# A decoder layer's MLP written as one row of 128 steps with every engine in a written order, operands loaded one by one, scaling and rectifier in one operation, and a fourth weight buffer in the output projection

## The chip, the core and the metric

The kernel runs on one core of a Trainium2 chip. The metric is device time in microseconds from launch to end, the median of several runs; lower is better. The core has a matrix engine (PE, TensorE), a vector engine (DVE, VectorE), an activation engine (ACT, ScalarE), a general engine (POOL, GpSimd) and a queue engine (SP) that here issues most transfers. Each takes its own instructions strictly in order; they wait for one another through semaphores. TensorE reads operands from on-chip memory and adds up in eight banks of PSUM; a bank must be emptied by another engine before a new sum starts in it.

## The reference

One layer of a hybrid decoder on 1024 positions of width 1024. Three branches (a matrix memory, differential attention, attention into 256 memory rows) make `merged`; the change lies behind them:

```python
x = x + merged @ w_out[l]
h2 = rms_norm(x, norm_mlp_g[l])
x = x + jnp.square(jax.nn.relu(h2 @ w_up[l])) @ w_down[l]
```

`w_up` is 1024 x 4096, `w_down` 4096 x 1024, everything float32.

## The kernel before, in words

Products are taken in a split float format: each float32 operand is kept as a high part (rounded by a cast on ACT) and a low part (the rest, a subtraction on DVE), and a product is three matmuls, high x high, high x low, low x high (`mm3`). A split of a tile is thus one ACT instruction and one DVE instruction behind it.

**Output projection** (end of `tail`'s first half, line 1410 on). Four groups of two output blocks; each group has two weight tiles of 128 x 1024 (`load_w`, line 142), cast and split into the pool `wp2`. Each of its four results is scaled and added to x (line 1416), stored to `x1d`, squared into `ssq` for the norm, and stored as `h` to `h2d`.

**The MLP** computes both matrix products by a scheme with seven products for a 2 x 2 block product in place of eight (`PROD`, line 1176). A *step* takes one weight block (2 x 2 blocks of 128 x 128) and one operand (2 x 2 blocks of 128 x 512): POOL makes four sums of weight blocks (`wino_s`), ACT and DVE split the seven weight forms (`wsp`), and TensorE runs 7 x 3 = 21 matmuls of 512 columns into seven banks. The operand's seven forms are four sums (`wino_t`, three on DVE and one on POOL) and three plain blocks, also split. Seven banks of eight are in use in a pass, and the next pass starts with the eighth (`bank`): from its second product on it needs the banks of the pass before, in their order.

The up-projection (`wino`) has 16 units of four steps; unit 0 is cut in two so that the MLP may start before the last operands exist. At the end of a unit the seven sums are combined into four results (`combine`: one ACT copy and seven DVE additions that read the banks); `use_up` scales each by the row norm (`tensor_mul`, line 1457), applies the rectifier (ACT, line 1458) and the square (ACT, line 1459), and stores the three plain blocks and, a step later, the four sums to `r_d`. The row norm itself is made inside the first steps by small matmuls (`rstd`; its copy `st`, line 1473, empties a bank that the next pass needs).

The down-projection (`down`) has four output groups and 16 passes of four steps, pass p for group p mod 4 with operands p to p+3; operands 16 to 18 are 0 to 2 loaded again, 19 loads in all. An operand is one to three tiles of 1024 to 2048 columns, each split by one ACT and one DVE instruction (`xsplit`). At the end of a pass the seven banks are added into seven accumulators (lines 1617 to 1619, 1637), and after a group's last pass seven more additions close the result, which is stored to `out`.

**What sets the order.** Matmuls of the MLP keep the written order (`self.pinned`). Everything else of the MLP (ACT, DVE, POOL, SP) was put in order by a planner at build time from its own estimates and the written order as priority. Weights have four raw buffers and four split buffers in the up-projection, three and three in the down-projection. The tiles of the down-projection take the memory of the up-projection's tiles as these come free, and those of the up-projection take that of the output projection's.

## Time and profile before

| what | value |
|---|---|
| median of 3 runs | 2248.64 us (2246.41 to 2258.45) |
| profiled execution: its own time | 2249.61 us |
| its span, first to last instruction | 2247.8 us |
| TensorE busy | 2182.6 us, 97% |
| DVE, ACT, POOL busy | 1398.3, 1019.8, 540.4 us |
| MLP on TensorE | from 1595.5 to 2243.8 us |
| mean granted clock of TensorE | 0.993 |

All numbers are from one profiled execution. In lists of instructions the columns are start, length, engine, source line, operation, tile written and tiles read, shape, count; in brackets the idle time of the engine just before and what ended it. In groups by line they are busy time and mean length (ns) of one, then idle time before them and what ended it. Tiles are named by the program: `p` the seven banks, `wo` split weights, `wraw` raw weights, `xo` and `xd` split operands of the up- and the down-projection, `xr` an operand as loaded, `xts` its sums, `acc` accumulators, `w` and `raw` the weights of the other projections. The lines of the helpers (91 matmul, 104, 105 and 115, 116 the split) stand for many places, so tiles are the better guide.

### The profile page before, as it was taken

How to read it: one execution, taken by the hardware profiler on the slowest of the kernel's cores; microseconds unless marked ns; L12 is line 12 of the kernel's file. 1: busy time of each engine (PE TensorE's matmuls, PEld its weight loads, DVE VectorE, ACT ScalarE, POOL GpSimd, SP SyncE). 2: the span in 40 equal slices, each digit the busy share in tenths (PEclk: the TensorE clock that was granted, in tenths of full speed). 3: DMA queues.
4: the chain of work that ended last, by engine and by line, in shares of the span. 5: the costliest groups of instructions: out<-in, count | busy, mean ns of one | idle time of the engine just before them, and what ended most of it. 6: DMA issues, size and time to landing. Idle time of an engine off the chain costs nothing.

```text
span 2247.8 us, 30530 instructions
## 1 busy us (share of the span) xinstructions
PE 2182.6 (97%) x11222; PEld 1877.5 (84%) x11222; DVE 1398.3 (62%) x2627; ACT 1019.8 (45%) x1994; POOL 540.4 (24%) x696
## 2 busy tenths in 40 slices
PE   7999899999999999999999999999899999899999
PEld 5778788988899999999888888887788888688777
DVE  6645366655138888888752232544588777865688
ACT  6533355444236666666542120323445444543232
POOL 2100000000011111111100002202666665665553
PEclk9999999999999999999999999999999999999999
DMA  6013122111311111110133443436445444844434
GB/s 246 20 71 113 44 87 78 54 60 52 119 55 34 34 31 38 38 36 29 61 128 135 134 148 117 141 103 206 153 143 186 151 155 162 296 163 147 154 118 169
DMA packets 113781, 247.89 MB, mean 110 GB/s; under 512 B 11066, under 2 KB 19551, under 8 KB 111583
## 3 DMA queue, kind: packets, MB, share of 16 engines
q1 hardware_dynamic: 111326, 233.36, 31.5%
q10 hardware_dynamic: 2304, 12.58, 1.4%
q8 instruction: 88, 1.44, 0.3%
q14 instruction: 63, 0.51, 0.1%
HBM read 178.76 MB, written 67.14 MB: 109 GB/s over the span
## 4 chain that ended last, share of the span: by engine, by line
PE 68%; DVE 14%; DMA 8%; ACT 5%; issue 2%; POOL 2%; SPq 0%; DVEq 0%; ACTq 0%; POOLq 0%
PE mm L91 40%; PE p L91 18%; PE sc L91 4%; PE tp L94 2%; PE po L91 2%; DVE sc L67 1%; DMA wraw<-in_wdown 1%; ACT dpe L67 1%; DVE wo L105 1%; DVE dpe L67 1%; PE pr L94 1%; DVE draw L67 1%; DVE dst L67 1%; DMA xr<-h_d 1%; DVE w L116 1%
## 5 line engine op out<-in xcount | busy, mean ns | idle before, releaser
L91 PE MATMUL mm<-hT,w 128*128 128x512 f32 x1920 | 466.4, 397 | 0.5 <-ACT gt L488 0.5
L91 PE MATMUL mm<-w,hT 128*128 128x384 f32 (+3 forms) x2496 | 459.3, 330 | 1.9 <-ACT w L115 1.6
L91 PEld LDWEIGHTS mm<-hT,w 128*128 128x128 f32 x1920 | 356.1, 189 | 76.0 <-ACT gt L488 1.7
L91 PEld LDWEIGHTS mm<-w,hT 128*128 128x128 f32 x2496 | 389.6, 189 | 12.1 <-ACT w L115 2.3
L91 PE MATMUL p<-xd,wo 128*128 128x512 f32 x1344 | 313.3, 394 | 16.5 <-DVE acc L1619 9.4
L91 PEld LDWEIGHTS p<-xd,wo 128*128 128x128 f32 x1344 | 253.5, 190 | 76.2 <-DVE acc L1619 12.8
L91 PE MATMUL p<-xo,wo 128*128 128x512 f32 x1344 | 309.5, 392 | 6.2 <-DVE st L1473 4.2
L91 PEld LDWEIGHTS p<-xo,wo 128*128 128x128 f32 x1344 | 253.2, 189 | 61.2 <-ACT pt L1286 4.6
L91 PE MATMUL mm<-kt,w 128*128 128x512 f32 x1152 | 261.8, 389 | 0.5 <-DVE w L116 0.5
L91 PEld LDWEIGHTS mm<-kt,w 128*128 128x128 f32 x1152 | 216.1, 188 | 46.1 <-DVE w L116 1.0
L104 ACT CAST wo<-wraw 128x896 fp32r<-128x896 f32 x122 | 114.9, 942 | 190.3 <-PE p L91 126.8
L105 DVE TENSOR_TENSOR wo<-wraw,wo 128x896 fp32r<-128x896 f32 x122 | 146.2, 1212 | 49.9 <-ACT wo L104 49.8
L1200 POOL TENSOR_TENSOR wraw<-wraw 128x128 f32<-128x128 f32 x128 | 99.0, 773 | 212.3 <-DMA wraw<-in_wdown 132.2
L115 ACT CAST w<-raw 128x256 fp32r<-128x256 f32 (+2 forms) x144 | 86.4, 619 | 140.1 <-PE mm L91 103.7
L67 ACT ACTIVATE dpe<-sc,dst,drr 128x256 f32<-128x256 f32 (+7 forms) x128 | 106.7, 833 | 62.2 <-DVE dst L67 51.6
L116 DVE TENSOR_TENSOR w<-raw,w 128x256 fp32r<-128x256 f32 (+2 forms) x144 | 100.5, 718 | 52.3 <-ACT w L115 52.3
L105 DVE TENSOR_TENSOR xd<-xd 128x1536 fp32r<-128x1536 f32 (+2 forms) x36 | 69.0, 1922 | 70.5 <-ACT xd L104 70.5
L67 DVE CUSTOM_DVE_ANT_0 sc<-sc,tmask 128x256 f32<-128x256 f32 (+7 forms) x128 | 97.0, 758 | 3.6 <-PE sc L91 2.4
L139 POOL TENSOR_SCALAR hss<-hss 128x4 f32<-128x4 f32 x8 | 3.3, 415 | 398.5 <-ACT mscr L767 398.5
L1201 POOL TENSOR_TENSOR wraw<-wraw 128x128 f32<-128x128 f32 x128 | 96.9, 757 | 0.0
L1202 POOL TENSOR_TENSOR wraw<-wraw 128x128 f32<-128x128 f32 x128 | 94.2, 736 | 0.0
L104 ACT CAST xd<-xd 128x1536 fp32r<-128x1536 f32 (+2 forms) x36 | 54.9, 1528 | 73.0 <-DMA xd<-r_d 73.0
(324 smaller groups left out, 3161.1 us busy)
## 6 DMA issues: line engine op xcount, KB each, us to landing
wraw<-in_wup SPq DMA_DIRECT2D x64, 256.0 KB, 3.2
r_d<-xts SPq DMA_DIRECT2D x16, 1024.0 KB, 4.3
wraw<-in_wdown SPq DMA_DIRECT2D x64, 256.0 KB, 3.1
xd<-r_d SPq DMA_DIRECT2D x19, 768.0 KB, 7.6
xd<-r_d SPq DMA_DIRECT2D x14, 1024.0 KB, 6.3
raw<-in_wgate SPq DMA_DIRECT2D x48, 256.0 KB, 3.0
gates<-gt SPq DMA_DIRECT2D x48, 256.0 KB, 2.1
raw<-in_wd SPq DMA_DIRECT2D x32, 384.0 KB, 3.1
```

Source lines behind the costliest of these rows:

```text
L67: return self.tc.keep_in_program_order(f(*a, **k))
L91: self.pin(self.nc.tensor.matmul(out, l, r, start=start, stop=stop))
L94: self.pin(self.nc.tensor.transpose(out, x, self.ident))
L104: self.A.copy(hi, src)
L105: low = lambda: self.V.tensor_sub(lo, src, f32(hi))
L115: nc.scalar.copy(hi, src)
L116: nc.vector.tensor_sub(lo, src, f32(hi))
L139: g.tensor_scalar(r, ss, 1.0 / width, EPS, op0=ALU.mult, op1=ALU.add)
L1200: G.tensor_add(r[:, 4], r[:, 0], r[:, 3])
L1201: G.tensor_sub(r[:, 5], r[:, 4], r[:, 1])
L1202: G.tensor_sub(r[:, 6], r[:, 1], r[:, 0])
```

## The change

- **One row of steps.** `wino`, `down` and their helpers go; one function `mlp` runs the 64 steps of the up-projection and the 64 of the down-projection in one loop with the same banks. All pools are opened at its start, with three split buffers and four raw buffers for weights, and the down-projection's tiles take over pools of the up-projection's by name.
- **Written order.** DVE, ACT, POOL and SP are wrapped in `InOrder` (line 57), which fixes the written order of what they do in the MLP. In step n the order is: the split of weight n+2, the load of raw block n+5, the sums of raw block n+4, then (inside a pass) the work listed for n and closing additions, or (at its end) the emptying of the banks, the work listed for n, closing additions. The first splits and operands 0 to 2 (`un`) are left to the planner.
- **Operands of the down-projection.** Passes get unequal lengths (`PASSES`): 19 passes of one to four steps, so that a new operand is first used every four steps or so and each of the 16 is loaded once. An operand is split in four pieces of two products (the last of one), four to two steps before its use; the load waits for the last use of the operand in its place, or, for the first five, stands at steps 44 and 60 to 63 (`nup` is 64).
- **Closing additions** (`fold`): two per step, 3 to 8 per step at the end.
- **Scaling with rectifier**: one `scalar_tensor_tensor` (maximum with 0, times the norm) for `tensor_mul` and the activation `Relu`. Unit 15's operand sums go to POOL wholly.
- **Output projection**: `wp2` has four buffers (three before), as a ring of named pools, as has `rp2`.
- A constant tile shrinks from 48 to 40 columns.

The core of the diff, new code first:

```diff
+    PASSES = (
+        (0, (0, 1)), (1, (0, 1)), (2, (0, 1, 2)), (3, (0, 1, 2, 3)),
+        (0, (2, 3, 4)), (1, (2, 3, 4, 5)), (2, (3, 4, 5, 6)), (3, (4, 5, 6, 7)),
+        (0, (5, 6, 7, 8)), (1, (6, 7, 8, 9)), (2, (7, 8, 9, 10)), (3, (8, 9, 10, 11)),
+        (0, (9, 10, 11, 12)), (1, (10, 11, 12, 13)), (2, (11, 12, 13, 14)),
+        (0, (13, 14, 15)), (1, (14, 15)), (2, (15,)), (3, (12, 13, 14, 15)),
+    )
...
+        V0, S0, A0, G0 = nc.vector, nc.sync, nc.scalar, nc.gpsimd
+        V, S, A, G = (InOrder(tc, e) for e in (V0, S0, A0, G0))
...
+        wrp, wop = Ring([wr0, wr1, wr2, wr3]), Ring([wop1, wop2, wop3])
...
+        def down_load(q):
...
+            for p_, tag, i, n in pools:
+                t = p_.tile([P, n, 2, 512], F32R, tag=tag, name=self.name("xd"))
+                for c0 in range(0, n, 4):
+                    c1 = min(c0 + 4, n)
+                    S.dma_start(f32(t[:, c0:c1, 1]), self.rd[q, :, i + c0 : i + c1])
+                parts[q] += [t[:, c0 : min(c0 + 2, n)] for c0 in range(0, n, 2)]
...
+        def down_split(q):
+            t = parts[q].pop(0)
+            split(t[:, :, 0], t[:, :, 1], f32(t[:, :, 1]))
...
+        at(nup - 20, lambda: down_load(0))
+        for i in (15, 15, 14, 11, 10):
+            at(nup - i, lambda: down_split(0))
+        for q in range(1, 16):
+            at(nup - 5 + q if q < 5 else n0[q - 4][-1], lambda q=q: down_load(q))
+            for i in (3, 2, 2, 2) if q == 1 else (4, 3, 2, 2):
+                at(n0[q][0] - i, lambda q=q: down_split(q))
+        for g, i in ((0, -8), (1, 1), (2, 4), (3, 8)):
+            at(nup + i, lambda g=g: acc_tiles(g))
...
+        def squares(u, cs):
+            b = hid[u] = xrp.tile([P, 4, 512], F32, tag="xr", name=self.name("rq"))
+            for i in (1, 3, 2, 0):
+                hf = i % 2
+                V.scalar_tensor_tensor(
+                    out=cs[i], in0=cs[i], scalar=0.0, in1=rb[:, hf * 512 : (hf + 1) * 512], op0=ALU.max, op1=ALU.mult
+                )
+                A.activation(b[:, i], cs[i], AF.Square)
+            A.dma_start(self.rd[u, :, 0:3], b[:, 1:4])
...
+        def fold(n):
+            if n >= nup + 57:
+                k = n - nup - 54 + (n >= nup + 60) - (n == nup + 58)
+            else:
+                k = 2
+            for _ in range(min(k, len(ends))):
+                f, x, y = ends.pop(0)
+                V.tensor_add(x, x, y)
+                if f:
+                    S.dma_start(f, x)
...
+                for i in range(len(run)):
+                    m = n - len(run) + 1 + i
+                    wsp()
+                    raw()
+                    wsum(m + 4)
+                if run[-1] != kps[-1]:
                     for f in todo.pop(n, []):
-                        next(f)
...
+                        f()
+                    if n > nup:
+                        fold(n)
...
+                    h = combine(ps, True)
+                    cs = next(h)
+                    next(h)
+                    k = 1 if r in (1, 3) or u == 15 else 0
+                    if k:
+                        at(n + 1, lambda u=u, cs=cs: squares(u, cs))
+                    else:
+                        squares(u, cs)
+                    at(n + 1 + k, lambda u=u: sums_up(u, G if u == 15 else V))
+                    at(n + 2 + k, lambda u=u: store(u))
...
+                if seen[g] == 1:
+                    V.tensor_sub(a3, a3, a5)
+                for j in range(7):
+                    if seen[g] == 1 and j in (0, 2, 3):
+                        A.copy(A_[j], ps[j])
+                    else:
+                        add(A_[j], A_[j], ps[j])
+            for f in todo.pop(n, []):
+                f()
+            fold(n)
...
-                    self.rp = E(name="rp2", bufs=2)
-                    self.wp = E(name="wp2", bufs=3)
+                    self.rp = Ring([E(name=f"rp2{i}", bufs=1) for i in range(2)])
+                    self.wp = Ring([E(name=f"wp2{i}", bufs=1) for i in range(4)])
...
-                        self.V.tensor_mul(cs[i], cs[i], rb[:, hf * 512 : (hf + 1) * 512])
-                        self.A.activation(cs[i], cs[i], AF.Relu)
-                        self.A.activation(b[:, i], cs[i], AF.Square)
...
-            passes = [(p % 4, tuple(range(p, 4 + p))) for p in range(16)]
...
+            self.mlp(one, gl, sp, rb, ssq, lambda *x, **k: c9.enter_context(tc.tile_pool(*x, **k)))
```

515 lines of the change are left out of this document (212 added, 303 removed).

## The prediction

> **What bounds the kernel now.** I read first the window table over the stages from the output projection to the end (columns: length, busy time and instruction count of each engine, granted clock, DMA share, GB/s), then what TensorE waited for, and last the order of time around each gap.
>
> ```profile
> 1520.00:1600.00 80.00, 75.44 (x331) 61.63 (x330) 35.90 (x35) 31.16 (x41) 25.84 (x20) 1.00 0.61 202
> 1600.00:1700.00 100.00, 93.84 (x415) 76.14 (x414) 84.65 (x100) 51.02 (x72) 72.37 (x88) 0.97 0.42 146
> 1700.00:1900.00 200.00, 200.00 (x884) 165.62 (x883) 160.86 (x195) 94.00 (x139) 124.55 (x179) 1.00 0.44 152
> 1900.00:1960.00 60.00, 52.07 (x212) 40.42 (x211) 47.76 (x44) 33.47 (x36) 28.88 (x33) 0.94 0.87 311
> 1960.00:2060.00 100.00, 100.00 (x442) 82.81 (x442) 62.86 (x61) 40.33 (x41) 62.98 (x85) 1.00 0.47 158
> 2060.00:2180.00 120.00, 114.11 (x497) 92.32 (x497) 81.43 (x88) 40.83 (x37) 63.90 (x92) 1.00 0.42 145
> 2180.00:2248.00 68.00, 61.07 (x260) 49.29 (x258) 56.75 (x70) 17.69 (x16) 26.72 (x43) 0.97 0.44 151
> ...
> 1872.20 0.58 ACT L1254 COPY u<-p 128x512 f32<-128x512 f32 x1
> 1891.24 0.57 ACT L1254 COPY u<-p 128x512 f32<-128x512 f32 x1
> ...
> L91 PE MATMUL px<-dg,ones 128*128 128x128 f32 x16 | 2.1, 274 | 0.0
> L91 PE MATMUL px<-ones,ssq 128*128 128x1 f32 x16 | 1.9, 246 | 0.0
> ...
> PE mm L91 <- DVE w L116: 4.6, 2, 3.0
> PE p L91 <- DVE acc L1619: 9.4, 8, 1.8
> ```
>
> TensorE bounds the kernel, so the change is worth the TensorE time now lost and no more. The two copies of one unit and the next lie 19.04 us apart; a unit is 4 steps of 21 matmuls, so a step takes 4.76 us and a matmul 0.2267 us. Unit for unit the second half of the up-projection and the window 1960 to 2060 run at that pace (442 matmuls per 100 us): nothing can be gained there. Against 442 per 100 us the other windows are short by: 1600 to 1700, 442 - (415 - 32 small ones) = 59 matmuls, 13.4 us, less 4.0 us that the small ones take, 9.4 us; 1900 to 1960 (full 266), 54, 12.2 us; 2060 to 2180 (531), 34, 7.7 us; 2180 to TensorE's end at 2243.8 (283), 23, 5.2 us. With the 4.6 us that the output projection waits for its weights this is 39.1 us, the most that can come back.
>
> **The change, part by part.** The sum is made against the profiled execution: 2249.6 us around a span of 2247.8; the median of the runs shown, 2248.6, is 1.0 lower.
>
> *Fourth out-projection buffer.* With three, the second weight tile of a group can be cast only when the tile three before is released, near the end of the group ahead, and then it stands behind an operand's long split:
>
> ```profile
> 1548.61 2.28 DVE L116 TENSOR_TENSOR xo<-xts,xo 128x2048 fp32r<-128x2048 f32 x1
> 1550.42 1.03 ACT L115 CAST w<-raw 128x1024 fp32r<-128x1024 f32 x1
> 1553.15 0.72 PE L91 MATMUL mm<-mh,w 128*128 128x512 f32 x2 [3.00 <-DVE w L116]
> ```
>
> With four the tile can be cast half a group, over 10 us, earlier, and both waits go: 4.6 us to 0 (bounds 0 and 4.6 left, should the planner still set the cast late). What hangs on the end of this stage, the last stores of h and the loads of the operands, moves with it.
>
> *Start, steps 0 to 5.* The bank that step 2 wants is held by the copy `st`, which stood behind the low parts of two weights, and those behind POOL's sums:
>
> ```profile
> 1609.94 1.09 DVE L105 TENSOR_TENSOR wo<-wraw,wo 128x896 fp32r<-128x896 f32 x1 [1.31 <-ACT wo L104]
> 1610.95 0.16 DVE L1473 COPY st<-px 128x8 f32<-128x8 f32 x1
> 1611.25 4.18 PE L91 MATMUL p<-xo,wo 128*128 128x512 f32 x9 [4.17 <-DVE st L1473]
> 1614.38 13.74 PE L91 MATMUL p<-xo,wo 128*128 128x512 f32 x56
> ```
>
> Nine matmuls took 3.1 us after that wait, 1.1 more than their 2.0. In the written order `st` follows only weight 2, whose raw buffer is now free early. The next wait is then the seven copies that empty the first pass: they stand behind the cast of weight 3 on ScalarE, which waits for a raw block whose buffer frees with the output projection. By the rows below, 3.1 us to land, 3.1 of sums, after POOL's last sums of squares, 0.9 and 0.6 for cast and copy make 8 to 12.5 us from the stage's end; it is wanted at 12. Of the 9.4 us in this window about 6 is the start (4.2 wait, 1.1 clock, rest small); I leave 1.5 (bounds 0.5 and 6). The remaining 3.4 us is VectorE's backlog over steps 5 to 19. Its work there is the same but for what is below; over steps 5 to 14 I count 10 low parts at 1.2, 21 combine and 7 part additions at 0.7, 12 scalings and 9 operand sums at 0.8, 48 us in 47.6. A pass end lets it run some 4 us behind, so I leave 2 (bounds 0 and 5).
>
> *Scaling with rectifier.* One scalar_tensor_tensor for a tensor_mul (its own form on two SBUF operands isn't in this trace; on a PSUM operand, below, it takes as long as an addition), and 64 activations of 632 ns, 40 us, leave ScalarE. They were off TensorE's path, hidden under the 200.00 us busy of 200: 0 (bounds -3 and 3: up to 0.2 us on 13 units). What it moves is the cast of the next weight, behind the last square: 0.6 us sooner.
>
> ```profile
> L105 DVE TENSOR_TENSOR wo<-wraw,wo 128x896 fp32r<-128x896 f32 x122 | 146.2, 1212 | 49.9 <-ACT wo L104 49.8
> L104 ACT CAST wo<-wraw 128x896 fp32r<-128x896 f32 x122 | 114.9, 942 | 190.3 <-PE p L91 126.8 <-POOL wraw L1203 45.8 <-POOL wraw L1200 3.8
> L1200 POOL TENSOR_TENSOR wraw<-wraw 128x128 f32<-128x128 f32 x124 | 96.1, 775 | 186.9 <-DMA wraw<-in_wdown 132.2 <-DMA wraw<-in_wup 46.3 <-DVE wo L105 3.2
> L1457 DVE TENSOR_TENSOR c<-c,rb 128x512 f32<-128x512 f32 x30 | 24.9, 829 | 0.5 <-ACT rb L1484 0.5
> L1458 ACT ACTIVATE c<-c 128x512 f32<-128x512 f32 x30 | 19.0, 632 | 61.8 <-DVE c L1457 61.8
> L1183 POOL TENSOR_TENSOR xts<-rq 128x512 f32<-128x512 f32 x16 | 28.1, 1755 | 49.6 <-ACT rq L1459 47.6 <-DMA r_d<-xts 2.0
> L105 DVE TENSOR_TENSOR xd<-xd 128x1024 fp32r<-128x1024 f32 x8 | 11.0, 1382 | 6.6 <-ACT xd L104 6.6
> L104 ACT CAST xd<-xd 128x1024 fp32r<-128x1024 f32 x8 | 8.4, 1049 | 10.1 <-DMA xd<-r_d 10.1
> L1642 DVE TENSOR_TENSOR acc<-acc,acc 128x512 f32<-128x512 f32 x3 | 2.0, 678 | 0.0
> xd<-r_d SPq DMA_DIRECT2D x19, 768.0 KB, 7.6
> wraw<-in_wdown SPq DMA_DIRECT2D x64, 256.0 KB, 3.1
> 2060.64 4.26 DVE L1619 TENSOR_TENSOR acc<-acc,p 128x512 f32<-128x512 f32 x7
> 1598.93 0.69 DVE L1416 SCALAR_TENSOR_TENSOR gl<-mm,gl 128x512 f32<-128x512 f32 x1 [4.05 <-DMA gl<-in_xT]
> ```
>
> *Seam.* Before, four operands (7.3 MB) with their splits come at once while the last unit is combined, at 311 GB/s and 12.2 us lost. Now operand 0 is loaded 20 steps and split 10 to 15 steps ahead, 1 to 4 are loaded over steps 60 to 63 and split in pieces of two products. DMA: steps 61 to 66 want 12.8 MB in 28.6 us; at 311 GB/s they take 41 us, so weights trail by up to 12 us. A raw block is issued three steps, 14.3 us, before its cast and needs 3 us on POOL, so ScalarE is held some 2 to 3 us at a cast, while TensorE's need comes two steps, 9.5 us, later: hidden. Not hidden is the first pass end after two steps. From step 63's start: low part and combine on VectorE to 7.4, three pieces of operand 1 to 10.7, low part 66 to 11.8, four scalings of unit 15 to 14.8. Its last square ends at 15.4, the cast of weight 67 at 16.4, and only then come the copies that empty pass 0: the first at 17.0, where step 66 wants the bank at 15.0 (2.1 late with its signal). The first addition (after low part and the subtraction) ends at 19.1, another 1.3 late: 3.4 us. In this trace such waits drop the clock in three places of four: the windows with 4.2, 1.9 + 1.8 and 2.1 us of waits show 0.97, 0.94 and 0.97 granted, while the 3.0 us wait of the output projection shows 1.00. In the second place 52 matmuls took 14.6 us for 11.8, and I add 2.0: 5.4 us in place of 12.2 (bounds 2 and 10). Unit 15's sums moved to POOL (4 at 1.755, 7 us, behind sums 69) delay weights 70 to 72 by that much and not past their need.
>
> ```profile
> 1919.42 1.20 PE L91 MATMUL p<-xd,wo 128*128 128x512 f32 x3 [1.92 <-DVE c L1258]
> 1922.43 14.59 PE L91 MATMUL p<-xd,wo 128*128 128x512 f32 x52 [1.81 <-DVE u L1260]
> 2185.17 27.06 PE L91 MATMUL p<-xd,wo 128*128 128x512 f32 x111 [2.09 <-DVE acc L1637]
> ```
>
> [...]
>
> *Middle of the down-projection.* Before, splits of 1536 and 2048 columns stand ahead of the additions that empty the banks (the eight waits for L1619). Now 16 operands are loaded instead of 19, four steps apart, and the emptying follows its step's low part directly. For four steps VectorE has 4 x 1.2 + 3 x 1.3 + 0.7 + 7 x 0.61 = 13.7 us of 19.0. Three more passes (19 for 16) are 21 more additions, 13 us, inside that slack. SP waits for TensorE's last use before each operand load, with the next raw block behind it: 7.6 + 3.1 us to landing and 3 on POOL is 13.7, before its cast at 14.3. I leave 1 of 7.7 (bounds 0 and 5).
>
> *End.* Three groups finish in steps 120, 122 and 123, with 21 additions and 18 of the 21 closing ones (0.68 each) ahead of the low part of weight 127:
>
> ```profile
> 2235.04 8.72 PE L91 MATMUL p<-xd,wo 128*128 128x512 f32 x37 [0.60 <-DVE wo L105]
> ```
>
> From step 122's start: cast and low part 124 to 2.2, seven additions to 6.5, three closing ones to 8.5, low part 125 to 9.6, seven to 13.9, five to 17.3, low part 126 to 18.4, seven to 23.2, low part 127 to 24.3. Steps 126 and 127 run as one, so TensorE wants it at 19.0 + 1.1 = 20.1: 4.2 us late by means, 2.8 at the shortest durations. I take 3.5 and 1.0 for the clock: 4.5 of 5.2 stays (bounds 1 and 8). The close after TensorE's end is unchanged.
>
> Sum left: 0 + 1.5 + 2 + 0 + 5.4 + 1 + 4.5 = 14.4; 39.1 - 14.4 = 24.7; 2249.6 - 24.7 = 2224.9, by the median 2224.
>
> **Rivals.** *Pass ends give it back:* 18 pass ends each wait like the eight before (9.4 / 8 = 1.2 us), 21.6 us where I have 6.4: 2239. For it: engines in a fixed order can't step round a late cast; against it: the 5 us a period of slack. *Slower:* in the up-projection the cast of a unit's fourth weight now always stands behind the four squares, and has three buffers instead of four. From the start of a unit's last step the chain is 12.2 us (low part, 7 combine steps, 4 scalings, square, cast, low part), need at 14.3, slack 2.1. If POOL's sums hold VectorE's two-operand work back more than the 829 ns row shows, each us over the slack costs 1 us on 13 units; from 2 us over, 26 us, it eats the gain, and at 3 over it gives 2224 + 39 = 2263. Against it: the unbroken 200 us, with the same VectorE work. *No loss left:* VectorE runs ahead everywhere but at the seam, 4 us left: 2249 - 35 = 2214, at best 2210. *The buffer and the start do nothing:* 4.6 + 4.5 more, 2233, inside my own range.
>
> **How the numbers follow.** Own case (2216 to 2234) 0.61, nothing left (below 2216) 0.13, pass ends (2234 to 2248) 0.19, slower 0.07. A change under 0.5%, 11 us, can't be told here. Faster than that is below 2237.4: 0.61 + 0.13 and a third of the pass ends, 0.80; same 0.13; slower 0.07. All low ends together leave 0.5 us (2210), all high ones 37 (2247), which doesn't happen at once; range 2210 to 2243.
>
> **What would show it.** No wait of `mm` for `w`; the copy `st` within 2 us of its small matmuls; the up-projection at 19.04 us a unit; the largest remaining wait of TensorE at step 66, behind the squares, and the next at the last weight's low part; no wait over 1 us between. Wrong, if a wait recurs once a unit, if the operands' DMA holds TensorE itself, or if the stalls at the pass ends add up to more than 10 us.

## The result

The changed kernel takes 2230.4 us (median of four, 2225.6 to 2233.3) where the kernel before takes 2249.6 (median of the four beside it): a ratio of 0.9911, 95% interval 0.9884 to 0.9938. The forecast was 2224 us with a range of 2210 to 2243. So the sign and the range held, and the gain is 19 us where 25 were forecast.

The profiled execution of the changed kernel happens to be its fastest, 2225.6 us around a span of 2223.7. That it meets the forecast to 2 us is luck. The first matmul of the output projection comes 5.9 us sooner in it than before (1497.3 for 1503.2), and over the eleven profiles with the same code ahead of it that moment lies anywhere from 1497.3 to 1504.5. The change reaches this earlier code at one point: `wp2` also holds the weights of the three branch projections ahead. With three buffers TensorE waits for these 0.5 us in before, 0.9 in e9 and 1.4 in e1 (both runs below); with four it doesn't wait. The rest of the 5.9 us is spread. So I compare lengths of stages, which don't carry that shift: the output projection, from its first matmul to the first one of the MLP; *up*, from there to the copy `u` of the last hidden unit in step 63; *down*, from that copy to TensorE's last matmul. The moments of before, first TensorE's and then ScalarE's:

```profile
1503.20 0.39 PE L91 MATMUL mm<-mh,w 128*128 128x512 f32 x1
...
1595.54 4.70 PE L91 MATMUL p<-xo,wo 128*128 128x512 f32 x20
```

```profile
1910.49 0.58 ACT L1254 COPY u<-p 128x512 f32<-128x512 f32 x1
```

And of after, with the rows that follow the MLP's first matmuls and the last one of TensorE:

```profile
1497.32 0.39 PE L91 MATMUL mm<-mh,w 128*128 128x512 f32 x1
...
1584.36 6.28 PE L91 MATMUL p<-xo,wo 128*128 128x512 f32 x27
1591.22 1.02 PE L91 MATMUL px<-pt_dg,ssq 128*128 128x1 f32 x8 [0.58 <-DVE gl L1629]
1593.92 1.05 PE L91 MATMUL px<-pt_dg,ssq 128*128 128x1 f32 x8 [1.68 <-POOL ssq L1636]
1594.83 5.51 PE L91 MATMUL p<-xo,wo 128*128 128x512 f32 x16
...
2209.25 10.32 PE L91 MATMUL p<-xd,wo 128*128 128x512 f32 x37 [3.14 <-DVE wo L67]
```

```profile
1898.62 0.57 ACT L67 COPY u<-p 128x512 f32<-128x512 f32 x1
```

| us | before | after | gained | forecast |
|---|---|---|---|---|
| output projection | 92.3 | 87.0 | 5.3 | 4.6 |
| up | 314.9 | 314.3 | 0.7 | 5.9 (start 4.5, steps 6 to 19 1.4) |
| down | 333.3 | 321.0 | 12.3 | 14.2 (seam 6.8, middle 6.7, end 0.7) |
| sum | | | 18.3 | 24.7 |

The 18.3 us agree with the 19.1 of the medians, and nearly all of what is missing is missing in up. The window table of after (length, busy time and count of TensorE, weight load, VectorE, ScalarE, POOL, then granted clock, DMA share, GB/s) and what TensorE waited for from 1480 us on:

```profile
1580.00:1600.00 20.00, 17.74 (x79) 14.43 (x79) 11.55 (x11) 9.90 (x14) 14.66 (x15) 0.91 0.67 227
...
1620.00:1640.00 20.00, 18.20 (x77) 13.73 (x76) 17.44 (x25) 7.00 (x10) 9.94 (x17) 1.00 0.24 84
1640.00:1660.00 20.00, 18.80 (x79) 14.10 (x78) 17.77 (x24) 5.64 (x8) 12.30 (x17) 1.00 0.41 145
...
1700.00:1900.00 200.00, 200.00 (x884) 165.61 (x883) 160.45 (x194) 72.86 (x101) 127.97 (x176) 1.00 0.50 176
1900.00:1920.00 20.00, 16.96 (x67) 13.30 (x66) 17.95 (x23) 9.27 (x14) 8.43 (x12) 0.92 1.04 397
...
1980.00:2180.00 200.00, 200.00 (x884) 165.62 (x883) 140.57 (x166) 74.85 (x84) 91.87 (x168) 1.00 0.44 148
```

```profile
PE p L91 <- DVE wo L67: 3.1, 1, 3.1
PE p L91 <- ACT acc L67: 1.7, 1, 1.7
PE px L91 <- POOL ssq L1636: 1.7, 1, 1.7
PE p L91 <- DVE pt_dg L67: 1.4, 1, 1.4
PE p L91 <- DVE acc L67: 1.3, 1, 1.3
...
PE p L91 <- DVE acc_xt L67: 0.8, 1, 0.8
...
```

The waits of `mm` for `w` are gone, and so are the eight for the old accumulators (their whole 9.4 us; 884 matmuls in 1980 to 2180 is full pace). The step that was forecast as the worst, 66, waits for exactly the two things named: a copy behind the squares (1.7 us, forecast 2.1) and an addition (1.3, forecast 1.3). The last weight's low part makes 3.1 us (forecast 3.5). But the first 80 us of the MLP are hardly better than before: waits for the norm's sum `ssq`, then a lower clock (0.50 granted from 1596 to 1599, and 16 matmuls in 5.5 us that take 3.6 at full pace), then waits between 1620 and 1660 while VectorE is busy for 17.4 to 17.8 us of every 20.

### The profile page after: what moved, and what is told of

Same layout as the page of the kernel before. It is cut to its first block, busy times and chain, and to the rows that moved or that the text cites. A ratio compares the mean times of both kernels' runs of the same rounds, so it can differ in the third digit from the quotient of the medians.

```text
span 2223.7 us, 30512 instructions
## 1 busy us (share of the span) xinstructions
PE 2175.5 (98%) x11222; PEld 1876.6 (84%) x11222; DVE 1392.2 (63%) x2667; ACT 975.3 (44%) x1952; POOL 508.3 (23%) x699
## 4 chain that ended last, share of the span: by engine, by line
PE 78%; DVE 10%; DMA 6%; ACT 4%; issue 1%; POOL 1%; SPq 0%; ACTq 0%; DVEq 0%; POOLq 0%
PE mm L91 44%; PE p L91 23%; PE sc L91 5%; PE tp L94 2%; PE po L91 2%; DVE sc L67 1%; ACT dpe L67 1%; DVE dpe L67 1%; DMA xr<-h_d 1%; PE pr L94 1%; DVE draw L67 1%; DVE dst L67 1%; DMA wraw<-in_wdown 1%; DVE u L67 1%; DMA h_d<-h 0%
## 5 line engine op out<-in xcount | busy, mean ns | idle before, releaser
L67 POOL TENSOR_TENSOR wraw<-wraw 128x128 f32<-128x128 f32 x496 | 316.4, 663 | 185.5 <-DMA wraw<-in_wdown 115.3
L67 DVE TENSOR_TENSOR wo<-wraw,wo 128x896 fp32r<-128x896 f32 x126 | 155.9, 1244 | 125.6 <-ACT wo L67 123.9
L105 DVE TENSOR_TENSOR w<-raw,w 128x256 fp32r<-128x256 f32 (+1 forms) x72 | 29.4, 436 | 87.9 <-ACT w L104 87.5
L91 PE MATMUL mm<-mh,w 128*128 128x512 f32 x256 | 79.0, 389 | 0.0
L91 PEld LDWEIGHTS po<-dv,daT 128*128 128x128 f32 x576 | 74.8, 189 | 0.9
L91 PE MATMUL po<-dv,daT 128*128 128x256 f32 x576 | 73.4, 271 | 0.0
```

Source lines behind the costliest of these rows:

```text
L67: return self.tc.keep_in_program_order(f(*a, **k))
L91: self.pin(self.nc.tensor.matmul(out, l, r, start=start, stop=stop))
L105: low = lambda: self.V.tensor_sub(lo, src, f32(hi))
```

## The experiments

Each run is the changed kernel with one edit unless it says otherwise. All lengths are from the one profile of each run, "whole" is the median with the ratio to before.

| run | whole, us | ratio (95%) | out-proj. | up | down |
|---|---|---|---|---|---|
| after | 2230.4 | 0.9911 (0.9884 to 0.9938) | 87.0 | 314.3 | 321.0 |
| e1 three buffers | 2231.6 | 0.9919 (0.9904 to 0.9934) | 92.5 | 310.3 | 322.3 |
| e2 closing additions later | 2227.1 | 0.9901 (0.9886 to 0.9916) | 87.0 | 316.2 | 316.1 |
| e3 last squares later | 2233.5 | 0.9932 (0.9915 to 0.9949) | 87.0 | 315.2 | 322.0 |
| e4 norm's matmuls later | 2230.9 | 0.9920 (0.9905 to 0.9934) | 87.0 | 315.5 | 321.5 |
| e5 unfused | 2254.3 | 1.0019 (1.0004 to 1.0034) | 87.0 | 339.4 | 323.9 |
| e6 no first combine | 2228.2 | 0.9905 (0.9883 to 0.9926) | 87.1 | 309.5 | 320.6 |
| e7 closing on POOL | 2227.1 | 0.9903 (0.9884 to 0.9923) | 87.0 | 311.5 | 322.5 |
| e8 last squares sooner | 2226.9 | 0.9901 (0.9881 to 0.9922) | 87.0 | 313.5 | 320.0 |
| e9 before, fused | 2248.0 | 0.9988 (0.9979 to 0.9998) | 92.4 | 315.3 | 334.7 |
| e10 first combine later | 2236.5 | 0.9937 (0.9923 to 0.9951) | 87.0 | 320.1 | 319.5 |
| e11 operands later | 2232.3 | 0.9920 (0.9907 to 0.9933) | 87.0 | 315.8 | 323.1 |
| e12 three edits | 2230.8 | 0.9913 (0.9897 to 0.9928) | 87.0 | 313.6 | 320.9 |

Six of these (after, e2, e3, e7, e8, e11) run the same instructions in up but for its last two steps: 311.5 to 316.2, mean 314.4. So a single length of up is good to some 2.5 us, no better.

### e1: three buffers again

```diff
-self.wp = Ring([E(name=f"wp2{i}", bufs=1) for i in range(4)])
+self.wp = Ring([E(name=f"wp2{i}", bufs=1) for i in range(3)])
```

> The change with the output projection's weights back in three buffers; all else as after. Theory (the forecast's first term): the projection waits for its weights again, 4.6 us in two or three waits of `mm` for `w`, so the stage from the first matmul of the output projection to the first of the MLP goes from 87.1 us back to 91.5 to 92.5 us, the MLP's 635.2 us stay, and the whole is 4.5 to 6.5 us longer than the changed kernel. Rival (the fourth buffer does nothing and the stage is shorter for another reason, for instance because the planner orders it differently): the stage stays within 1 us of 87.1 us and no such wait comes back.

The stage went to 92.5 us and the waits came back (0.3 us, then 3.0 us at 1551.5, with 0.81 of the clock granted from 1547 to 1556), so the fourth buffer does make those 5.5 us. Yet the whole is only 1.1 us longer by the medians. What TensorE waited for in e1, and its first matmuls of the MLP:

```profile
PE mm L91 <- DVE w L116: 3.0, 1, 3.0
```

```profile
1593.65 6.28 PE L91 MATMUL p<-xo,wo 128*128 128x512 f32 x27
...
1599.79 1.81 PE L91 MATMUL px<-pt_dg,ssq 128*128 128x1 f32 x15
1601.47 17.99 PE L91 MATMUL p<-xo,wo 128*128 128x512 f32 x78
```

With three buffers the small `px` matmuls wait for nothing, the clock stays up (78 matmuls in 18.0 us), and up takes 310.3 us, 4.1 less than the mean of the six. The reason lies in VectorE's and the DMA's rows around the end of the projection. In after, the last tile of `x` arrives 6.0 us after the MLP's first matmul (`gl` at 1590.38); in e1, 2.3 us after it:

```profile
1581.13 0.69 DVE L1240 TENSOR_TENSOR xts<-xr 128x512 f32<-128x512 f32 x1 [7.43 <-DMA xr<-h_d]
...
1584.31 1.28 DVE L1629 SCALAR_TENSOR_TENSOR gl<-mm,gl 128x512 f32<-128x512 f32 x2
...
1590.38 0.69 DVE L1629 SCALAR_TENSOR_TENSOR gl<-mm,gl 128x512 f32<-128x512 f32 x1 [0.96 <-DMA gl<-in_xT]
```

```profile
1586.59 0.69 DVE L1240 TENSOR_TENSOR xts<-xr 128x512 f32<-128x512 f32 x1 [7.51 <-DMA xr<-h_d]
...
1589.77 1.27 DVE L1629 SCALAR_TENSOR_TENSOR gl<-mm,gl 128x512 f32<-128x512 f32 x2
1595.91 0.69 DVE L1629 SCALAR_TENSOR_TENSOR gl<-mm,gl 128x512 f32<-128x512 f32 x1 [4.87 <-DMA gl<-in_xT]
```

The tiles of `x` go through two buffers, so the last fetch can start only when the additions on the tiles before it are done. Those additions (1584.31, 1589.77) stand in VectorE's order behind the sums of an operand (`xts`), and the sums wait for that operand's load from `h_d`. Behind the load the distances are nearly fixed: 3.2 us from the first sum to the two additions, about 6.1 from these to the last one, then its square and POOL's sum. The load, not TensorE, thus sets when the norm's sum is ready. Counted from the first matmul of the projection, the load is in 85.5 us on in e1 and 83.8 in after: 1.7 us sooner, where TensorE is 5.5 us sooner at the end of the stage. The MLP waits for the difference.

How much comes back varies, as the load does: in the eleven profiles with four buffers it lands 5.9 to 9.5 us after its issue. Of the six above, e7 has it in 5.4 us ahead of the MLP's first matmul, waits 0.5 us for `px` and has the shortest up (311.5); e2 has it in 2.6 us ahead, waits 3.0 us and has the longest (316.2). Against the single up of e1, 1 to 6 of the 5.5 us thus come back as waits for `px` and lost clock, 4 in the mean of the six.

### e2 and e7: the closing additions

e2 put the closing additions behind the low part of weight 127:

```diff
-                k = n - nup - 54 + (n >= nup + 60) - (n == nup + 58)
+                k = {57: 3, 58: 3, 59: 5, 60: 2}.get(n - nup, 8)
```

> The change with the closing additions that stand in steps 121 to 124 ahead of the low part of weight 127 moved behind it (3, 3, 5, 2 of them in the last steps before it, the rest after); nothing is left out. Theory (the forecast's end term): VectorE's order alone makes TensorE wait 3.14 us for that low part and run its next matmuls at a lower clock; the wait falls under 0.5 us, the last 37 matmuls take 8.4 to 8.9 us in place of 10.3, and TensorE's last matmul comes 4 to 4.7 us sooner after the start of the MLP; the whole gains 3 to 4.7 us, as at most a few of the moved additions then stand behind TensorE's end. Rival (the additions only change places and the close after TensorE's end grows by as much): TensorE ends 4 us sooner but the whole is the same within 1 us. Second rival (the low part waits for ScalarE's cast, not for the additions): the wait stays over 2 us.

The wait went (107 matmuls without a break at the end), TensorE ended down in 316.1 us, 4.8 sooner. Then VectorE worked on to 2223.9, 4.6 us after TensorE's last matmul, where in after it ends 1.1 us after it. From 2191.75 on it has no gap in e2 until its end:

```profile
2209.51 1.08 DVE L67 TENSOR_TENSOR wo<-wraw,wo 128x896 fp32r<-128x896 f32 x1
...
2211.12 2.01 DVE L67 TENSOR_TENSOR acc_xt<-acc_xt 128x512 f32<-128x512 f32 x3
```

So by the lengths in the two profiles the first rival held: the wait was real and in the place forecast, but VectorE's amount of work bounds the end, and its order hardly matters. From the up copy to VectorE's end is 322.0 us in after and 320.7 in e2, 1.3 us less. The median of e2 is 3.3 us lower, as the theory had it; the intervals can tell neither from nothing. The next run took work away from VectorE:

```diff
-                k = n - nup - 54 + (n >= nup + 60) - (n == nup + 58)
+                k = {57: 3, 58: 4}.get(n - nup, 8)
...
-                V.tensor_add(x, x, y)
+                (V if n < nup + 59 else G).tensor_add(x, x, y)
```

> The change with 14 of the 21 closing additions (all of the second and the third group that finish) on the POOL engine in place of VectorE, the seven of the first group on VectorE in steps 121 and 122; nothing is left out. Theory (VectorE's amount of work at the end is the bound, and moving it within VectorE, as in the second run, only pushes it past TensorE's end; POOL has none from 2200 us on): the wait of 3.1 us for the low part of weight 127 goes, the clock stays up, the work after TensorE's last matmul stays at 4.1 to 4.5 us in place of the 7.65 us of the second run, and the whole is 3 to 4.5 us shorter than the changed kernel. Rival (POOL at 1.755 us an addition, 24.6 us for the 14 from about 2192 us on, slows VectorE or ends last): VectorE's additions there take over 0.8 us in place of 0.68, or the last store waits for POOL, and the whole gains under 1.5 us.

The wait for the low part went here too, and another of 4.9 us took its place, for additions that empty a bank. VectorE and POOL in e7:

```profile
2189.62 0.68 DVE L67 TENSOR_TENSOR acc<-acc,p 128x512 f32<-128x512 f32 x1
2190.22 6.17 DVE L67 TENSOR_TENSOR acc<-acc,acc 128x512 f32<-128x512 f32 x4
2196.31 2.15 DVE L67 TENSOR_TENSOR wo<-wraw,wo 128x896 fp32r<-128x896 f32 x1
```

```profile
2188.22 1.30 POOL L67 TENSOR_TENSOR c<-c,u 128x512 f32<-128x512 f32 x1
```

Beside POOL's additions, VectorE's additions of two SBUF tiles take 1.54 us each (6.17 for four) in place of 0.67 (2.01 for three, in e2 above), a low part 2.15 in place of 1.08, while those with an operand in PSUM keep their 0.6 to 0.7 (1.28 for two from 2188.43 on, beside the POOL row above). So neither way of moving the closing additions gives a gain that can be told: 0.9901 and 0.9903 against 0.9911.

### e3, e8, e11: the seam

e3 put the last unit's squares, its scalings with them, two steps later, and the accumulators of two groups one step later; e8 put the squares one step sooner; e11 left them and spread the operands' loads.

```diff
 e3   -                    k = 1 if r in (1, 3) or u == 15 else 0
      +                    k = 3 if u == 15 else 1 if r in (1, 3) else 0
      +                        at(n + 3, lambda u=u, cs=cs: (squares(u, cs), acc_tiles(1)))
      -        for g, i in ((0, -8), (1, 1), (2, 4), (3, 8)):
      +        for g, i in ((0, -8), (2, 5), (3, 8)):
 e8   -                    k = 1 if r in (1, 3) or u == 15 else 0
      +                    k = 1 if r in (1, 3) else 0
      -            for i in (3, 2, 2, 2) if q == 1 else (4, 3, 2, 2):
      +            for i in (3, 3, 2, 2) if q == 1 else (4, 3, 2, 2):
 e11  -            at(nup - 5 + q if q < 5 else n0[q - 4][-1], ...
      +            at((60, 62, 66, 70)[q - 1] if q < 5 else n0[q - 4][-1], ...
```

> The change with the four scalings and squares of the last hidden unit two steps later (step 66 in place of 64), its sums and store two steps later as well, and the accumulators of the second and third group allocated one step later; nothing is left out. Theory (the forecast's seam term): the two waits at step 66, 1.73 and 1.31 us, come from these squares and scalings standing ahead of the copy and the additions that empty the first pass; they go, the clock stays up, 1900 to 1920 goes from 67 matmuls to 80 or more, and the MLP is 3.5 to 5.5 us shorter. Rival (the traffic of the seam, 397 GB/s in this window, holds the weights back and the waits only move): waits of the same sum, 2.5 us or more, come back within the next 8 steps, behind the late squares or at a weight, and the MLP is within 1.5 us of 635.2.

> The change with the four scalings and squares of the last hidden unit one step sooner (right behind its combine, like those of the units ahead of it) and the second piece of operand 1 split one step sooner; nothing is left out. Theory (the order on VectorE and ScalarE makes the two waits at step 66, not the traffic): the squares end some 4 us sooner, the copies that empty the first pass stand free, both waits (1.7 and 1.3 us) go; in exchange the last pieces of operand 1 come up to 1.1 us late at step 65; the MLP is 1.5 to 4 us shorter. Rival (the raw block of weight 67 is late because of the traffic, as its cast in the third run waited 6.85 us for POOL's sums): the copies then stand behind that cast in any order and at least 1.5 us of wait stays at step 66, or the pieces of operand 1 wait 2 us or more at step 65; the MLP is within 1.5 us of the changed kernel's.

> The change with the loads of operands 2, 3 and 4 of the down-projection at steps 62, 66 and 70 in place of 61, 62 and 63; nothing is left out. Traffic theory (the third and the eighth run moved the waits at the seam instead of removing them, so it is the 395 GB/s of four operands in 20 us that makes weights and pieces late): 1900 to 1920 falls to 330 GB/s or less, the casts of weights 66 to 68 come 2 us or more sooner, the waits of TensorE between 1900 and 1980 (4.6 us in sum) fall under 2.5 us, and the MLP is 2 to 4 us shorter. Order theory (the forecast: the squares of the last hidden unit ahead of the copies at step 66): the traffic falls, but the waits at step 66, 1.7 to 1.9 and 1.0 to 1.4 us, stay within 0.4 us of that, only the later ones (0.78 and 0.76 us, behind loads of accumulators) shrink, and the MLP is 0 to 1.5 us shorter.

In e3 the two waits at step 66 fell to 0.3 us, as the theory had it, and 0.6 and 5.4 us turned up two steps on. The squares hold the tiles that the next accumulators are loaded into, so VectorE's first operation on them waits for a late DMA:

```profile
1933.34 1.52 DVE L67 TENSOR_TENSOR acc<-acc,acc_rb 128x512 f32<-128x512 f32 x1 [3.57 <-DMA acc_rb<-x_d]
```

In e8 the waits at step 66 went as well, and came back as 1.2 and 0.8 us for pieces of operand 1 one step earlier, and 1.0 and 1.4 us at step 68, where the copy `u` stands behind a cast that waited 6.85 us for POOL's sums of a late raw block. ScalarE in e8:

```profile
1926.54 0.94 ACT L67 CAST wo<-wraw 128x896 fp32r<-128x896 f32 x1 [6.85 <-POOL wraw L67]
1927.39 1.06 ACT L67 COPY u<-p 128x512 f32<-128x512 f32 x2
```

In e11 the traffic of 1900 to 1920 fell from 397 to 295 GB/s (286 from 1905.6 to 1925.6, the same stretch counted from the copy `u`), and the waits at step 66 did not: 1.85 and 1.96 us. So the two waits come from the order on ScalarE and VectorE, as forecast, and not from the traffic; but behind them stand others of about the same sum, some from late blocks and loads, and the best of the three has down at 320.0 us, 1.0 shorter than after.

### e4 and e12: the start

```diff
 e4   -  if (r, q, j) in ((0, 1, 1), (1, 1, 6), (1, 2, 6), (1, 3, 3)):
      +  if (r, q, j) in ((0, 1, 5), (1, 1, 6), (1, 2, 6), (1, 3, 3)):
 e12  as e8, and   (0, 1, 1) -> (0, 1, 3)
      -  at(n + 1, lambda u=u, cs=cs: squares(u, cs))       with k = 2 for r == 1
      +  at(n + k, lambda u=u, cs=cs: squares(u, cs))
      -  G.tensor_add(ssq[:, s], ssq[:, s], q)
      +  (V if f == 7 else G).tensor_add(ssq[:, s], ssq[:, s], q)
```

> The change with the 16 small matmuls that sum the squares of h for the norm issued four products (12 matmuls, 2.7 us) later in step 1; nothing is left out. Theory: at the start TensorE waits 0.58 and 1.68 us for the last addition of squares on the POOL engine because these matmuls stand too early in its order, and then runs 16 small matmuls at half clock (5.5 us in place of about 2); with 2.7 us more both waits go, the clock stays up, and steps 0 to 5 lose under 1 us in place of 3.8 us: the MLP is 2.5 to 4 us shorter. Rival: what is late is the fetch of the last tiles behind the output projection, and something else waits for it next (the copy of the sums, then the bank it holds, or the first weights): the wait moves behind the small matmuls, 1 us or more on the copy `st`, and the MLP is within 1.5 us of 635.2.

> The change with three edits that touch three different stretches, so that each can be read by itself; nothing is left out. Start: the last two additions of squares on VectorE (0.7 us by its rows) in place of POOL (2.0), and the small matmuls two products (1.4 us) later. Early units: the second unit's scalings and squares one step later, behind the seven additions that empty the third pass (the tenth run, which was meant to do this too, moved only their sums and store, so the wait of 1.38 us was not tested by it). Seam: as in the eighth run. Theory: at the start the 0.6 and 1.7 us of waits fall under 0.5 us and POOL's sums for weight 3 come 2 us sooner; the 1.38 us wait goes; the seam as in the eighth run (4.3 us of waits between 1900 and 1935, no gain); together the MLP is 3 to 4.5 us shorter than the 635.2 us and the whole takes 2225 to 2228 us. Rival (every wait removed at the start and in the early units is only passed to the next copy or low part, as VectorE's backlog is what is late): waits over 1 us turn up on the copy `st`, on the copies that empty the first pass, or in steps 8 to 16; the MLP is within 1.5 us and the whole 2229 to 2232 us.

e4 took the waits for `ssq` down to 0.2 us and got 1.04 and 0.93 us in their place, for the copy `st` and for the copies that empty the first pass, with 0.50 of the clock granted from 1600 to 1605: the rival held. The forecast's own chain is what stands there. In e4 the copies wait for the cast of weight 3, and that for POOL:

```profile
1600.01 0.94 ACT L67 CAST wo<-wraw 128x896 fp32r<-128x896 f32 x1 [3.69 <-POOL wraw L1224]
1600.85 1.55 ACT L67 COPY pt_dg<-p 128x512 f32<-128x512 f32 x3
```

In e12 nothing waits for `ssq` or `st` and the clock stays up (1.00 granted from 1580 to 1620), but the copies that empty the first pass still make 1.2 us, and in the early units the 1.38 us wait gave way to 2.7 us for the copy `u` behind unit 0's squares. Again the rival: up 313.6, whole 2230.8.

### e5 and e9: the fused operation

```diff
 e5   -                V.scalar_tensor_tensor(
      -                    out=cs[i], in0=cs[i], scalar=0.0, in1=rb[...], op0=ALU.max, op1=ALU.mult
      -                )
      +                V.tensor_mul(cs[i], cs[i], rb[...])
      +                A.activation(cs[i], cs[i], AF.Relu)
 e9   the reverse of this, in the kernel before
```

> The change with the scaling and the rectifier apart again, as before: a multiplication on VectorE and an activation on ScalarE for each of the 64 tiles, in the new order; nothing is left out. Theory (the forecast's term of 0): the activations are off TensorE's path, so units 3 to 14 stay at 19.04 us each (442 matmuls per 100 us from 1700 to 1900), ScalarE is 40 us busier, and only where the squares stand ahead of a copy (seam, early units) 0.2 to 1.5 us come on top: the MLP 635 to 638 us. Rival (the forecast's slower case turned round: the chain of a unit's end is near its slack of 2.1 us, and the fused form is what keeps it there): with 4 times 0.2 to 0.6 us more per unit a wait comes back once a unit, and the MLP is 645 us or more.

> The kernel before with one edit: scaling and rectifier as one scalar_tensor_tensor, its order still planned; nothing is left out. After the fifth run (the change without the fused form took 2254 us, a wait in every unit), two theories of the fused form are left. A (it is worth something only in the new order: there the cast of a unit's fourth weight stands behind four activations and four squares, and the planned order lets that cast go ahead of them): before with the fused form is within 5 us of before's 2249 us and units 3 to 14 stay at 19.04 us. B (the fused form alone is worth the 20 us, whatever the order, and the rest of the change gives nothing): it comes to 2230 to 2235 us. In the trace of before the second half of the up-projection had no loss, so A is the likelier, 9 to 1.

This is the result that the forecast had not seen. Without the fused form the whole change is worth nothing (1.0019, 1.0004 to 1.0034), and the fused form alone, in the order of before, takes 1.7 us off before (2248.0 for 2249.7, 0.9979 to 0.9998). Up is 25 us longer in e5. TensorE in e5 waits at least once in every unit (1716.70 to 1796.76 are four units, 20.02 us each):

```profile
1716.70 19.38 PE L91 MATMUL p<-xo,wo 128*128 128x512 f32 x84 [0.45 <-DVE wo L67]
...
1796.76 19.35 PE L91 MATMUL p<-xo,wo 128*128 128x512 f32 x84 [0.67 <-DVE wo L67]
```

One unit's end on ScalarE in e5, and the same in after:

```profile
1782.26 0.58 ACT L67 COPY u<-p 128x512 f32<-128x512 f32 x1
1789.52 0.63 ACT L67 ACTIVATE c<-c 128x512 f32<-128x512 f32 x1 [6.69 <-DVE c L67]
...
1794.28 2.60 ACT L67 CAST wo<-wraw 128x896 fp32r<-128x896 f32 x3
```

```profile
1784.38 0.57 ACT L67 COPY u<-p 128x512 f32<-128x512 f32 x1
1791.39 1.23 ACT L67 ACTIVATE rq<-c 128x512 f32<-128x512 f32 x2 [6.44 <-DVE c L67]
...
1793.74 1.77 ACT L67 CAST wo<-wraw 128x896 fp32r<-128x896 f32 x2
```

From the copy `u` to the cast of the weight that stands behind the squares: 12.0 us in e5, 9.4 in after. With the low part behind it (1795.24 + 1.46, and 1794.70 + 1.46 on VectorE) the weight is ready 14.4 and 11.8 us after the copy. In e5 TensorE wants it at 1796.09 (1796.76 less its wait), 13.8 after the copy: 0.6 late, and 2.0 early in after. VectorE's four scalings take the same in both (1.29 us for two), so it is the four activations that make it late. That is the chain of the forecast's slower rival, whose slack it gave as 2.1 us. Of the 25 us that up is longer in e5, 7 are lost at the eight such waits from 1716.7 to 1856.2. Of the rest, 10 are lost ahead of these, with a longest wait of 3.8 us at 1640.7, and 8 behind them, where two units that also split operand 0 wait 2.0 and 2.1 us.

In the planned order of before the same eight activations cost nothing. There the next cast goes ahead of six of them:

```profile
1796.04 0.58 ACT L1254 COPY u<-p 128x512 f32<-128x512 f32 x1
1799.40 0.63 ACT L1458 ACTIVATE c<-c 128x512 f32<-128x512 f32 x1 [2.78 <-DVE c L1457]
...
1800.65 0.93 ACT L104 CAST wo<-wraw 128x896 fp32r<-128x896 f32 x1
1802.90 0.63 ACT L1458 ACTIVATE c<-c 128x512 f32<-128x512 f32 x1 [1.33 <-DVE c L1457]
```

Its weight is ready 9.9 us after the copy (the low part runs from 1804.81 to 1805.89), against 14.4 in e5. But the order is not the only difference. Before has four split buffers in the up-projection and splits three steps ahead; the change has three and splits two steps ahead, so that e5 wants the weight a step, 4.76 us, earlier than before does. By an estimate from these rows either of before's two would have been enough: 9.9 us is under e5's 13.8, and 14.4 is under 13.8 + 4.76. So the activations stand in the weights' way where the written order and the smaller number of split buffers come together; no run takes the two apart.

### e6 and e10: the early units

e6 leaves out the seven additions that combine the first unit, and scales four raw products in their place. e10 moves the additions five steps later, and that unit's squares seven.

```diff
 e6   -  h = combine(part, False)          (and its two steps)
      +  c0 = [part[i] for i in (0, 1, 2, 4)]
 e10  -  at(n + 1, lambda h=h: c0.extend(next(h)))
      -  at(n + 2, lambda h=h: next(h))
      -  at(n + 3, lambda: squares(0, c0))
      ...
      +  at(n + 6, lambda h=h: c0.extend(next(h)))
      +  at(n + 7, lambda h=h: next(h))
      +  at(n + 10, lambda: squares(0, c0))
      ...
      -  k = 1 if r in (1, 3) or u == 15 else 0
      +  k = 2 if r == 1 else 1 if r == 3 or u == 15 else 0
```

> The change without the seven additions that combine the first unit's products (four of the raw products are scaled, rectified and squared in place of the four combined sums, so this unit's hidden values are not the reference's); all else is done. Theory: the waits of TensorE between 1650 and 1660 us (0.55, 0.64 and the copies behind them) come from VectorE, which has 17.4 to 17.8 us of work in every 20 between 1620 and 1680 and runs behind; with 4.9 us of additions gone these waits fall to under 0.5 us, steps 6 to 19 lose 3 us or less in place of 5.6, and the MLP is 2 to 3 us shorter. Rival (the order on ScalarE alone makes them: copies behind squares and casts): they stay within 0.5 us of what they are.

> The change with the first unit's seven combine additions moved from steps 8 and 9 to steps 13 and 14, its scalings and squares from step 10 to 17, its sums and store behind them, and the second unit's squares from step 6 to step 7, behind the additions that empty the third pass; nothing is left out. Theory (the backlog of VectorE over steps 5 to 14 makes the waits of 1.38, 0.64 and 0.43 us and two smaller ones; the sixth run without those additions lost only the first two waits): the 1.38 us wait and the two around step 14 go, the losses of steps 6 to 19 fall from 5.6 to 1.5 us or less, and the MLP is 2.5 to 4 us shorter than 635.2, the whole by as much. Rival (the additions only wait for the next step in which VectorE is full): waits of 2 us or more in sum turn up in steps 13 to 20 and the MLP is within 1.5 us.

In e6 there is no wait from 1640 us to the seam, so VectorE's backlog does make those around 1655 (0.64 and 0.43 us in after, and smaller ones); the 1.38 us wait stays, which is that of additions behind the second unit's squares. Up is 309.5 us, 2.0 shorter than in e7, whose start is like e6's (`px` waits 0.5 and 0.2 us). In e10 the waits around 1655 went likewise, but 0.5 and 3.25 us turned up at 1701 to 1705, and up, 320.1 us, is longer than in any of the six. (The move of the second unit's squares that this expectation names is not in e10: its edit moved only their sums and store. It is in e12, where the 1.38 us wait is gone.) ScalarE in e10 shows why a backlog is not cured by moving work to where there is room:

```profile
1695.45 0.63 ACT L67 ACTIVATE rq<-pt_dg 128x512 f32<-128x512 f32 x1 [5.45 <-DVE pt_dg L67]
...
1698.54 1.77 ACT L67 CAST wo<-wraw 128x896 fp32r<-128x896 f32 x2
1700.21 0.57 ACT L67 COPY u<-p 128x512 f32<-128x512 f32 x1
```

The copy is due at 1694.8 (the ones before it are at 1656.76 and 1675.80, 19.04 apart) and comes at 1700.2: ScalarE's queue holds it behind four extra squares, and the first of these waits 5.45 us for VectorE.

## Why the prediction was right, and where it was wrong

**Bound and whole.** TensorE bounds the kernel, and what came back is TensorE's lost time: right. The range and the sign are right; the size is 6.4 us short of the forecast. The forecast's high ends add up to 41.6 us, not 37: the buffer's 4.6 is missing, and with it the high end would be 2251. Nothing measured comes near it.

**Fourth buffer.** The term itself was right (4.6 forecast, 5.3 in the stage, 5.5 when undone). The step that failed is the sentence behind it, that what hangs on the end of the stage "moves with it". It doesn't: the norm's sum hangs on the load of an operand and on VectorE's order behind it, which came 1.7 us sooner where TensorE came 5.5 sooner, so about 4 us of the gain are given back at the MLP's start. The net worth of the buffer is 1.1 us by the medians of e1 and after; their intervals can tell that neither from nothing nor from the 4.6 that the sum booked.

**Start and steps 6 to 19.** This is the largest error: 5.9 us forecast, 0.7 measured (0.5 by the mean of the six). The forecast named the copies of the first pass as the next to be late; ahead of them stood the norm's small matmuls, which it did not look at, and the clock that their waits cost (0.50 granted from 1596 to 1599). The copies are next indeed (e4, e12). With three buffers, where the norm's chain is in time, up is 4.7 us shorter than before (314.9 to 310.3), near the forecast. For steps 6 to 19 the forecast had VectorE's work right, 48 us in 47.6, and took the backlog for nearly harmless; e6 shows that 4.9 us less work there makes the waits around 1655 vanish, and e10 that the backlog outlasts those steps.

**Scaling with rectifier.** Forecast 0, and its reason was the unbroken 200 us of before, an order that the change gives up. e9 confirms it for the old order, e5 refutes it for the new one: 24 us between 2254.3 and 2230.4. The step that failed is to cost the part against the old kernel, when other parts of the same change (the order and the number of split buffers) move it onto the path. The forecast had the chain, its length and its slack in its slower rival, and did not work out that chain without the fused form.

**Seam.** The waits at step 66 were right in place, cause (e11 against traffic) and size (1.73 and 1.31, forecast 2.1 and 1.3). From 1900 to 1980, 323 matmuls ran where 353 fit, 6.8 us lost; 5.4 were forecast here and 1 in the middle. The forecast let the operands come at 311 GB/s; they came at 397.

**Middle.** 1 left of 7.7 was forecast; 1980 to 2180 runs at full pace and 0.8 us are lost at 1963. That the new passes and the order took the old waits away is read from the two traces; no run undoes either alone.

**End.** Forecast 3.5 and 1.0 of clock; 3.14 measured, and 37 matmuls in 10.32 us, 1.6 over the 8.72 that the same 37 took in before. What the forecast left out is that VectorE is the bound right behind, so that by the lengths little of this wait can be won by order (1.3 us in e2, none in e7).

**Rivals.** "Pass ends give it back" fell: no wait of the middle is over 0.8 us. "Slower" did not happen, but its mechanism is real and 2.0 us away. "The buffer and the start do nothing", 2233, is nearest to what was measured for the whole, and in part for the reason: together they gave 6.0 us before the MLP's last unit where 10.5 were booked. It had been put inside the own range and given no chance of its own.

**No better version.** e2, e7 and e8 have medians 3.3 to 3.5 us below after, but their ratios (0.9901 to 0.9903) lie well inside after's interval. What stays open is how much of the spread of up, 311.5 to 316.2 us with the same instructions, is the norm's chain alone: the waits for it were 0.5 to 3.0 us in those profiles, and why the operand's load takes 5.9 us in one and 9.5 in another wasn't tried.

## What to carry to other kernels

Cost each part of a change in the kernel that the other parts leave behind: here one fused instruction is worth 1.7 us in the old kernel and 24 in the new one, because a fixed order with fewer buffers turns hidden work on a second engine into work that stands ahead of a weight. When a stage is made shorter, follow what its last outputs feed: a chain that hangs on a load and on another engine's order does not move up with TensorE, and about 4 of 5.5 us came back in the next stage. And before a wait is moved by order, add up the work of the engine that causes it up to the end: where that engine is full, or a late load stands behind, the wait only changes its place (e2, e3, e4, e8, e10, e12).

## What was not expected of the hardware

**One wait, many prices.** The wait for the low part of weight 127 is 3.13 to 3.15 us in ten of these profiles, and the 37 matmuls behind it take 8.68, 8.69, 9.97, 10.24, 10.28, 10.31, 10.32, 11.39, 11.53 and 11.57 us. The two ends:

```profile
2210.64 8.68 PE L91 MATMUL p<-xd,wo 128*128 128x512 f32 x37 [3.14 <-DVE wo L67]
```

```profile
2215.76 11.57 PE L91 MATMUL p<-xd,wo 128*128 128x512 f32 x37 [3.15 <-DVE wo L67]
```

The first, of e8, is full pace (1.00 granted from 2210 to 2220; in before the same 37 took 8.72 us behind a wait of 0.60), the second, of e11, had 0.74 granted from 2215 to 2228. So the same wait of 3.1 us at the same place in the program costs from nothing to 2.9 us of clock on top. The 3.0 us wait of the output projection differs likewise: 1.00 granted from 1549 to 1558 in before, 0.81 from 1547 to 1556 in e1. And at after's start two waits of only 0.6 and 1.7 us, with eight one-column matmuls between them, are followed by 16 matmuls in 5.5 us that take 3.6 at full pace, with 0.50 granted from 1596 to 1599. What sets the price of a wait is not shown by these rows.

**Two engines on SBUF.** In e7, beside POOL's additions, VectorE's additions of two SBUF tiles took more than twice as long as in e2 (1.54 us for 0.67), while those from PSUM kept their 0.6 to 0.7.

**Code that isn't changed moves.** The same instructions ahead of the output projection end up to 7.2 us apart (1497.3 to 1504.5) from one profiled execution to another, so that one profile against one profile can show or hide a third of this change.
